# SSD decay matrices of a two-layer diffusion backbone: from rank-8 matmuls into PSUM to broadcast rows in SBUF

## The chip, the cores and the metric

The kernel runs on one core of a Trainium2 chip. The metric is the device time of one execution in microseconds; three runs of the kernel before gave a median of 1857.68 us (1857.05 to 1858.12). The profiled execution, from which all durations below come, took 1859.69 us, and its span from the first to the last instruction is 1858.0 us.

## The reference, cut to what matters

The model has two layers on 1024 latent and 256 context tokens of width 1024: layer 0 is windowed attention, layer 1 a bidirectional state-space mixer (SSD) with 8 groups of 4 heads of 64 and a state of 128. Only layer 1's scan is touched. For each direction, head and chunk of 128 tokens:

```python
a_cs = jnp.cumsum(da, axis=2)                        # running sum of dt * A inside a chunk
diff = a_cs[:, :, :, None] - a_cs[:, :, None, :]     # (query token q, source token s)
lmat = jnp.exp(jnp.where(lower, diff, -jnp.inf))     # decay from s to q, s <= q
cb = jnp.einsum('bcqgn,bcsgn->bcqsg', cm, bm)
y_diag = jnp.einsum('bcqsg,bcqsgr,bcsgrp->bcqgrp', cb, lmat, xdt)   # xdt = x * dt
y_off = jnp.einsum('bcqgn,bcgrpn,bcqgr->bcqgrp', cm, h_prev, jnp.exp(a_cs))
```

The backward direction does the same on the flipped sequence. The kernel puts both directions into one 128 x 128 matrix per head, with the source token on the partitions: where s is not after q the entry is exp(acs_f[q] + v_f[s]), elsewhere exp(acs_b[q] + v_b[s]), with v = ln(dt) - acs. Multiplied by cb this is M, and M times x gives y_diag of both directions.

## The kernel before, in words

Layer 0 fills about the first 755 us of the span, layer 1 the rest. Layer 1 starts with the constants (`ssd_consts`): dt for all 64 head-directions in two sets (768 and 512 tokens), the running sums `acs` by two scans on VectorE, `v`, and per chunk some small transposes by TensorE (lines 956, 959, 960) that ScalarE copies out (957, 961, 962). `rows()` splits `acs` and `v` each into a rounded high part (cast on ScalarE, 929) and the rest (subtraction on VectorE, 930), so that fp32r matmuls keep the precision, and SyncE stores both parts to DRAM (932).

Then comes the scan. 8 groups times 8 chunks are 64 slots, about 13.8 us each. A slot does the work of one chunk; between its steps `fill(0)` to `fill(4)` issue the projections of the next group (TensorE lines 1046, 1055, 1080, with weight loads on SyncE at 991, their split at 995 on ScalarE and 999 on VectorE), or in the last group the output projection. Beside that runs the chain of states of the next group (`states`: POOL xw 1130, TensorE 1153, POOL decay 1135, VectorE add 1165). The program is written in this order, but the order on each engine is set before the run by a list scheduler that models durations; on the chip each engine then takes its instructions strictly in that order, and a DMA is issued by SyncE in the place where the schedule has it.

The decays of a slot are made one slot ahead. `load_rows` reads 8 rows of acs and 16 of v (three small DMAs, 1176 and 1178) into `rraw`, of which there is one; `round_rows` casts it to fp32r on ScalarE (1181) and then loads the next. `decays` runs for two heads at a time: two matmuls (1189) with constant selecting rows give acs[q] + v[s] of both directions in one PSUM tile (`psX`, three buffers), VectorE copies the backward half over the forward half where `before` says so (1190), ScalarE takes the exponential (1191) into M. In the slot itself VectorE multiplies M by pcb (1205) and four matmuls use it (1230). Of the rest of a slot, these matter: POOL's xs and y (1225 to 1227) and the power (1242), the tail's transposes (1258) and their store uN (1260).

Of the kernel before, what the change touches and what calls it, by code (L numbers as in the profile page):

```python
# [9 lines left out]
F32 = mybir.dt.float32  # L10
BF16 = mybir.dt.bfloat16
F32R = mybir.dt.float32r
AF = mybir.ActivationFunctionType
ALU = mybir.AluOpType
# [3 lines left out]
P = 128  # L18
D = 1024
KT = D // P  # L20
LAT = 1024
# [11 lines left out]
G = 8  # L33
R = 4
HP = 64
NST = 128
NCH = LAT // P
# [5 lines left out]
    pj=1, S=2, pt=2, pv=1,  # L43
    rope_b=2, qf=3, qh=3, ql=2, kHH=2, kLL=2, qs=2, sgt=2, sm=7, mx=2, nm=2, es=2, sums=2, ph=2, pl=2, co=1, ot=2,
    oraw=3, h1=2, h1k=8, wada=8, sqa=1,
    cacc=2, cctx=1, bT=2, cT=2, xn4=4, xn2=1, bn4=4, bn2=1, sz=2, xw=2, hf=2, hx=2, M=2, y2=1, xs=1, uT=2, pj2=2, psX=3, sk=2, dg=2,
)
VLAST = 0
G0 = 6
# [54 lines left out]
class Kernel:  # L104
# [13 lines left out]
    def t(self, pool, shape, dt, tag, bufs=None):  # L118
        self.n += 1
        kw = {"bufs": bufs or BUFS.get(tag, 1)}  # L120
        return pool.tile(shape, dt, tag=tag, name=f"{tag}_{self.n}", **kw)
# [727 lines left out]
    def ssd_consts(self, p):  # L849
        nc, t, a = self.nc, self.t, self.a  # L850
        ps = self.psA
        NT = NCH + NCC
        dr = self.dr
# [12 lines left out]
        self.eacs = t(p, [P, NCH, 64], F32, "eacs")  # L866
        self.dtdec = t(p, [P, NT, 64], F32, "dtdec")
        self.dtb = t(p, [P, NCH, 32], F32, "dtb")
        self.eal = t(p, [P, 64, NT], F32, "eal")

        self.acs_d = t(dr, [2, 64, LAT], F32, "acs")
        self.v_d = t(dr, [2, 64, LAT], F32, "vrow")
        self.before = t(p, [P, P], mybir.dt.int32, "before")
        nc.vector.memset(self.before, 1)
        nc.gpsimd.affine_select(out=self.before, in_=self.before, pattern=[[-1, P]], compare_op=ALU.is_gt, fill=0, base=0, channel_multiplier=1)
# [1 line left out]
        q = self.pdt  # L877
# [19 lines left out]
        for i in (2, 0, 1):  # L897
            n = TT[i][1]
            pj = self.proj(ps, (wh, wl), i, tag="psX", m=64)
            nc.scalar.activation(dts[:, where[i] : where[i] + n], pj[:64, :n], AF.Identity, bias=db)  # L900
        for lo, n, chunks in ((0, 768, (0, 1, 2, 3, 8, 9)), (768, 512, (4, 5, 6, 7))):
            nb = n // P
            dt = dts[:, lo : lo + n]
            if lo:
                q = self.pool("dtp2", ctx=self.cdt, side="right")
            w1, w2, w3 = [t(q, [64, n], F32, x) for x in ("w1", "w2", "w3")]

            nc.vector.scalar_tensor_tensor(w1, in0=dt, scalar=-1.0, in1=dt, op0=ALU.mult, op1=ALU.min)
            nc.scalar.activation(w1, w1, AF.Exp)
            nc.vector.tensor_scalar_add(w2, w1, 1.0)  # L910
            nc.vector.tensor_scalar_add(w3, w2, -1.0)
            nc.vector.tensor_sub(w1, w1, w3)
            nc.scalar.activation(w2, w2, AF.Ln)
            nc.scalar.activation(w3, w2, AF.Exp, scale=-1.0)
            nc.vector.tensor_mul(w1, w1, w3)
            nc.vector.tensor_add(w1, w1, w2)
            nc.vector.scalar_tensor_tensor(dt, in0=dt, scalar=0.0, in1=w1, op0=ALU.max, op1=ALU.add)
            ln = w2
            nc.vector.tensor_scalar_max(ln, dt, 1.0e-38)
            nc.scalar.activation(ln, ln, AF.Ln)  # L920
            da = w1
            nc.vector.tensor_scalar(out=da, in0=dt, scalar1=al, scalar2=None, op0=ALU.mult)
            acs = w3
            nc.vector.tensor_tensor_scan(out=acs[:32], data0=keep[:32, :n], data1=da[:32], initial=0.0, op0=ALU.mult, op1=ALU.add)
            nc.vector.tensor_tensor_scan(out=acs[32:, ::-1], data0=keep[32:, :n][:, ::-1], data1=da[32:, ::-1], initial=0.0, op0=ALU.mult, op1=ALU.add)
            def rows(dst, src):
                h = t(q, [64, 512], F32R, "rowh", 2)
                l = t(q, [64, 512], F32R, "rowl", 2)
                nc.scalar.copy(h, src[:, :512])
                nc.vector.tensor_sub(l, src[:, :512], h)  # L930
                for x, y in enumerate((h, l)):
                    nc.sync.dma_start(dst[x, :, chunks[0] * P : chunks[0] * P + 512], y.bitcast(F32))

            rows(self.acs_d, acs)
            av = acs.rearrange("p (c n) -> p c n", n=P)
            tot = t(q, [64, 6], F32, "tot")[:, :nb]
            nc.vector.tensor_copy(tot[:32], av[:32, :, P - 1])
            nc.vector.tensor_copy(tot[32:], av[32:, :, 0])
            et = t(q, [64, 6], F32, "et")[:, :nb]
            nc.scalar.activation(et, tot, AF.Exp)  # L940
            nc.sync.dma_start(eal_d[0][:, chunks[0] : chunks[0] + 4], et[:, :4])
            if nb > 4:
                nc.sync.dma_start(eal_d[0][:, 8:10], et[:, 4:])

            nc.vector.tensor_sub(ln, ln, acs)
            rows(self.v_d, ln)

            dd = w1
            nc.vector.tensor_sub(dd.rearrange("p (c n) -> p c n", n=P), tot.unsqueeze(2).broadcast_to([64, nb, P]), av)
            nc.scalar.activation(dd, dd, AF.Exp)  # L950
            nc.vector.tensor_mul(dd, dd, dt)
            nc.scalar.activation(acs, acs, AF.Exp)
            for b, c in enumerate(chunks):
                sl = slice(b * P, (b + 1) * P)
                pt = t(ps, [P, 256], F32, "psX")
                nc.tensor.transpose(pt[:, 0:64], dd[:, sl], self.ident[:64, :64])
                nc.scalar.copy(self.dtdec[:, c, :], pt[:, 0:64])
                if c < NCH:
                    nc.tensor.transpose(pt[:, 64:128], acs[:, sl], self.ident[:64, :64])
                    nc.tensor.transpose(pt[:, 128:192], dt[:, sl], self.ident[:64, :64])  # L960
                    nc.scalar.copy(self.eacs[:, c, :], pt[:, 64:128])
                    nc.scalar.copy(self.dtb[:, c, :], pt[:, 160:192])
        nc.sync.dma_start(self.eal, eal_d.broadcast_to([P, 64, NT]))

    def taps(self, x, raw, acc, lo, hi, n):
# [130 lines left out]
    def ssd(self, c0):  # L1096
        nc, t, a = self.nc, self.t, self.a
        ps = self.psA
# [6 lines left out]
        ps2 = self.pool("scan", ctx=c0)  # L1105


        rraw = t(ps2, [32, 6, P], F32, "rraw")
        rrow = t(ps2, [P, 6, P], F32R, "rrow")
        nc.sync.dma_start(rraw, a["rrow"].rearrange("p (r n) -> p r n", r=6))  # L1110
        nc.vector.memset(rrow.bitcast(F32), 0.0)
        ys = []
        for x in range(2):
            y = t(ps2, [P, 260], F32, f"y{x}")
# [4 lines left out]
        def hd(d, g):  # L1119
            return slice(32 * d + 4 * g, 32 * d + 4 * g + 4)  # L1120
# [48 lines left out]
                        st["hb"][o] = h = hn  # L1169
                yield  # L1170

        def load_rows(n):
            g, c = divmod(n, NCH)
            cs = slice(c * P, (c + 1) * P)
            ar = self.acs_d.rearrange("h (d k) n -> (h d) k n", d=2)[:, 4 * g : 4 * g + 4, cs]
            nc.sync.dma_start(rraw[0:4, :4], ar)
            for d in range(2):
                nc.sync.dma_start(rraw[4 + 8 * d : 12 + 8 * d, 4 + d], self.v_d[:, hd(d, g), cs])

        def round_rows(n):  # L1180
            nc.scalar.copy(rrow[:32], rraw)
            if n + 1 < G * NCH:
                load_rows(n + 1)

        def decays(n, M, half):

            o = t(ps, [P, 512], F32, "psX").rearrange("p (d r n) -> p d r n", d=2, r=2)
            for d in range(2):
                nc.tensor.matmul(o[:, d], rrow[:, 4 + d], rrow[:, 2 * half : 2 * half + 2], start=True, stop=True)
            nc.vector.copy_predicated(o[:, 0], self.before.unsqueeze(1).broadcast_to([P, 2, P]), o[:, 1])  # L1190
            nc.scalar.activation(M[:, 2 * half : 2 * half + 2], o[:, 0], AF.Exp)

        def slot(n, st, M, fill, tick, last):

            g, c = divmod(n, NCH)
            cs = slice(c * P, (c + 1) * P)
            xc = X(st, c).rearrange("p (r h) -> p r h", r=R)
            if n + 1 < G * NCH:
                round_rows(n + 1)
            pcb = t(ps, [P, 512], F32, "psX")[:, :P]  # L1200
            nc.tensor.matmul(pcb, st["bT"][:, cs], st["cT"][:, cs], start=True, stop=True)
            po = t(ps, [P, 512], F32, "psX")
# [28 lines left out]
            if self.tail is not None:  # L1231
                self.tail(t(ps, [P, 512], F32, "psX"))
            fill(1)
            nM = None
            if n + 1 < G * NCH:
                nM = t(ps2, [P, R, P], F32, "M")
                decays(n + 1, nM, 0)
            nc.vector.tensor_add(yv, yv, yd[:, :256].rearrange("p (r h) -> p r h", r=R))
            nc.vector.tensor_mul(yf, yf, st["sz"][c])
            ss = t(ps2, [P, 1], F32, "ss", 2)  # L1240
            nc.scalar.activation(y2.rearrange("p d r h -> p (d r h)")[:, :257], y[:, :257], AF.Square, scale=1.0 / 16.0, accum_out=ss)
            nc.gpsimd.tensor_tensor(ss, ss, self.half, op=ALU.pow)
            fill(2)
            if nM is not None:
                decays(n + 1, nM, 1)
            nc.scalar.activation(yf, yf, AF.Copy, scale=ss)
            if c < NCH - 2:
                st["xw"] = xweight(st, g, c + 1, 0)
# [15 lines left out]

        post = Queue()
        st = {}
        load_rows(0)
        done = 0.0
        chain = None
        for cost in self.front(0, st, post):  # L1270
# [8 lines left out]
        post.flush()  # L1279
        for _ in chain:  # L1280
            pass
        M = t(ps2, [P, R, P], F32, "M")
        round_rows(0)
        for half in range(2):
            decays(0, M, half)
        st["xw"] = xweight(st, 0, 0, 0)
        self.tail = None
        with ExitStack():
            for g in range(G):
# [25 lines left out]
                for c in range(NCH):  # L1315
                    def fill(x):
                        run(total * (c + sum(SEGS[: x + 1]) / sum(SEGS)) / NCH)
# [233 lines left out]
def layout(i):  # L1551
# [31 lines left out]
    rm = np.where(k > q, np.float32(NEG), np.float32(0))  # L1583
    z = np.zeros((P, P), np.float32)

    rr = np.zeros((32, 6, P), np.float32)
    for x in range(4):
        for r in range(R):
            rr[4 + 4 * x + r, r] = 1.0
        rr[x, 4 + x % 2] = 1.0  # L1590
    d["rrow"] = rr.reshape(32, -1)
    d["mask"] = np.concatenate([lm, z, rm, z, z, lm, z, z, z], 1).astype(np.float32)
    w = i["ssd_w_in"][0]
    d["w_z"] = np.ascontiguousarray(w[:, :SW].reshape(2, 4, P, G, 256).transpose(3, 0, 2, 1, 4)).reshape(G, 2, P, 1024)
# [27 lines left out]
```

## Time and profile before

| | before |
|---|---|
| median of 3 runs | 1857.68 us |
| profiled execution, its span | 1859.69 us, 1858.0 us |
| TensorE busy, share of the span | 1778.6 us, 96% |
| VectorE, ScalarE, GpSimd busy | 63%, 49%, 39% |
| mean granted TensorE clock | 0.988 |
| DMA traffic | 196.30 MB, 106 GB/s |

PE is TensorE's matmul, PEld its weight load, DVE VectorE, ACT ScalarE, POOL GpSimd, SP (or SPq) SyncE, which issues most DMAs. A row of a group reads: line, engine, operation, output<-input, shape, count | busy us, mean ns of one | idle us of the engine just before them, and what ended it. Matmuls are pipelined, so a matmul's duration is longer than the distance to the next one; what it costs TensorE is that distance, from the starts in the timeline.

### The profile page before, as it was taken

How to read it: one execution, taken by the hardware profiler on the slowest of the kernel's cores; microseconds unless marked ns; L12 is line 12 of the kernel's file. 1: busy time of each engine (PE TensorE's matmuls, PEld its weight loads, DVE VectorE, ACT ScalarE, POOL GpSimd, SP SyncE). 2: the span in 40 equal slices, each digit the busy share in tenths (PEclk: the TensorE clock that was granted, in tenths of full speed). 3: DMA queues.
4: the chain of work that ended last, by engine and by line, in shares of the span. 5: the costliest groups of instructions: out<-in, count | busy, mean ns of one | idle time of the engine just before them, and what ended most of it. 6: DMA issues, size and time to landing. Idle time of an engine off the chain costs nothing. (4 is left out here: it accounts for less than half of the span.)

```text
span 1858.0 us, 29740 instructions
## 1 busy us (share of the span) xinstructions
PE 1778.6 (96%) x10684; PEld 1537.0 (83%) x10684; DVE 1176.4 (63%) x2208; ACT 902.9 (49%) x1858; POOL 731.7 (39%) x1007
## 2 busy tenths in 40 slices
PE   6999999999999998979999999999999999999997
PEld 4797877788898786768898898989889898988886
DVE  3654438777778666773766657576665757754743
ACT  3522336677788664552444435344443534543532
POOL 2441137654466454103252443525344352542411
PEclk9999999999999999989999999999999999999998
DMA  7767866443355447021111111111111111433552
GB/s 294 278 170 251 272 167 151 106 116 97 90 136 121 127 129 229 17 65 35 30 40 52 33 47 33 48 33 39 53 34 47 34 47 34 155 109 98 176 161 72
DMA packets 145492, 196.30 MB, mean 106 GB/s; under 512 B 15393, under 2 KB 84897, under 8 KB 144321
## 3 DMA queue, kind: packets, MB, share of 16 engines
q1 hardware_dynamic: 111280, 175.76, 30.2%
q0 software_dynamic: 34064, 18.65, 5.5%
q8 instruction: 84, 1.38, 0.3%
q14 instruction: 64, 0.52, 0.1%
HBM read 158.73 MB, written 35.92 MB: 105 GB/s over the span
## 5 line engine op out<-in xcount | busy, mean ns | idle before, releaser
L226 PE MATMUL pj<-uH,wh 128*128 128x256 f32 (+1 forms) x664 | 236.9, 357 | 5.7 <-DVE xn L1510 1.9
L228 PE MATMUL pj<-uH,wl 128*128 128x256 f32 (+1 forms) x664 | 224.5, 338 | 2.0 <-POOL wl L214 2.0
L227 PE MATMUL pj<-uL,wh 128*128 128x256 f32 (+1 forms) x664 | 224.1, 337 | 0.4 <-POOL uL L720 0.4
L1130 POOL TENSOR_TENSOR xw<-xn,dtdec 128x256 f32<-128x256 f32 x144 | 105.9, 738 | 205.4 <-PE psD L1153 102.9
L214 POOL TENSOR_TENSOR wl<-wr,wh 128x512 fp32r<-128x512 f32 x100 | 132.1, 1324 | 109.7 <-ACT wh L212 103.6
L1055 PE MATMUL pj<-uH,wh 128*128 128x512 f32 x512 | 171.7, 405 | 1.3 <-ACT xn L1022 1.3
L1055 PE MATMUL pj<-uH,wl 128*128 128x512 f32 x512 | 171.5, 404 | 0.0
L1055 PE MATMUL pj<-uL,wh 128*128 128x512 f32 x512 | 168.6, 399 | 0.0
L1080 PE MATMUL pj<-wh,uH 128*128 128x256 f32 x512 | 154.7, 302 | 0.0
L702 DVE TENSOR_TENSOR pl<-pt,ph 128x512 fp32r<-128x512 f32 x168 | 114.3, 688 | 59.7 <-ACT ph L701 58.9
L1080 PE MATMUL pj<-wh,uL 128*128 128x256 f32 x512 | 151.2, 295 | 0.0
L1080 PE MATMUL pj<-wl,uH 128*128 128x256 f32 x512 | 150.9, 295 | 0.0
L226 PEld LDWEIGHTS pj<-uH,wh 128*128 128x128 f32 x664 | 126.3, 190 | 28.8 <-issue 7.8
L212 ACT CAST wh<-wr 128x512 fp32r<-128x512 f32 (+1 forms) x140 | 89.8, 643 | 106.2 <-PE pj L227 78.1
L228 PEld LDWEIGHTS pj<-uH,wl 128*128 128x128 f32 x664 | 125.9, 190 | 17.7 <-POOL wl L214 3.2
L676 DVE CUSTOM_DVE_ANT_0 sm<-S,mask,nsink 128x640 f32<-128x640 f32 (+2 forms) x160 | 119.0, 772 | 33.7 <-PE S L673 19.7
L1259 ACT ACTIVATE uT<-psX,nw 128x128 f32<-128x128 f32 x128 | 47.0, 367 | 189.7 <-PE psX L1258 188.6
L227 PEld LDWEIGHTS pj<-uL,wh 128*128 128x128 f32 x664 | 126.6, 191 | 11.3 <-issue 1.1
L701 ACT CAST ph<-pt 128x512 fp32r<-128x512 f32 x168 | 97.6, 586 | 60.9 <-PE pt L697 54.9
L678 ACT ACTIVATE sm<-sm,nm 128x640 f32<-128x640 f32 (+2 forms) x160 | 118.5, 742 | 17.4 <-DVE nm L676 14.6
L1225 POOL TENSOR_TENSOR xs<-xn,sk 128x256 f32<-128x256 f32 x64 | 42.1, 657 | 185.1 <-DVE sk L1221 183.8
L1055 PEld LDWEIGHTS pj<-uL,wh 128*128 128x128 f32 x512 | 95.6, 188 | 19.9
(332 smaller groups left out, 5022.6 us busy)
## 6 DMA issues: line engine op xcount, KB each, us to landing
wr<-w_x SPq DMA_DIRECT2D x32, 512.0 KB
wr<-wo SPq DMA_DIRECT2D x48, 256.0 KB
wr<-w_sk SPq DMA_DIRECT2D x24, 512.0 KB
wr<-wg SPq DMA_DIRECT2D x44, 256.0 KB
qs<-q POOLq DMA_DIRECT2D x40, 256.0 KB, 3.9
wada<-w_ad SPq DMA_DIRECT2D x8, 1024.0 KB
wr<-wq SPq DMA_DIRECT2D x32, 256.0 KB
wl<-w_ada SPq DMA_DIRECT2D x32, 256.0 KB
```

The source lines that it names most:

```text
L212: nc.scalar.copy(h, raw)
L214: (eng or nc.vector).tensor_tensor(l, raw, h, op=ALU.subtract)
L226: self.nc.tensor.matmul(ps, lh, rh, start=first and i == 0, stop=False)
L227: self.nc.tensor.matmul(ps, lh, rl, start=False, stop=False)
L228: self.nc.tensor.matmul(ps, ll, rh, start=False, stop=last and i == n - 1)
L676: nc.vector.tensor_tensor_reduce(out=sm[:, :W], in0=Sv, in1=self.mask[:, m0 : m0 + W], scale=-SCALE, scalar=self.nsink[:, 4 * j + r : 4 * ...
L678: nc.scalar.activation(sm[:, :W], sm[:, :W], AF.Exp, bias=nm[:, r : r + 1], scale=-1.0, accum_out=sums[:, r : r + 1])
L701: nc.scalar.copy(ph, ptf)
L702: nc.vector.tensor_sub(pl, ptf, ph)
L1055: nc.tensor.matmul(raw[:, 512 * i : 512 * i + 512], l[:, k, :], r[i][:, k, :], start=k + y == 0, stop=k == KT - 1 and y == 2)
L1080: nc.tensor.matmul(pj[:, c], l, r[:, k, :], start=c % 2 + q + k + y == 0, stop=c % 2 == 1 and q == 1 and k == 3 and y == 2)
L1130: nc.gpsimd.tensor_tensor(xw, X(st, c).rearrange("p (r h) -> p r h", r=R), self.dtdec[:, c, hd(d, g)].unsqueeze(2).broadcast_to([P, R, HP] ...
```

## The change

The running sums are stored to DRAM unsplit, v is not stored, and `rows()` is gone with its casts, subtractions and its second and third stores per set. The constants get one more transpose per latent chunk (8 in all, line 955 in the new file), of v: the forward part is copied to `vf` by ScalarE (956), and `vo` = v_b - v_f is formed by VectorE (957).

For each slot two DMAs of 256 KB now bring four rows of acs (512 B each), repeated on all 128 partitions: `fd` forward (two buffers, issued two slots ahead, in the program right after `fill(1)`) and `bd` backward (one buffer, issued one slot ahead, right after the exponentials of the slot before). GpSimd adds vo to bd in place (`offset`, 1173); one copy_predicated of 128 x 512 in SBUF puts bd over fd (1178); four exponentials of 128 x 128, one per head, with vf as the bias of each partition, finish M in place in fd (1180). The matmuls of 1189, the selecting rows, the casts of 1181 and the two PSUM tiles a slot are gone.

```diff
-    cacc=2, cctx=1, bT=2, cT=2, xn4=4, xn2=1, bn4=4, bn2=1, sz=2, xw=2, hf=2, hx=2, M=2, y2=1, xs=1, uT=2, pj2=2, psX=3, sk=2, dg=2,
+    cacc=2, cctx=1, bT=2, cT=2, xn4=4, xn2=1, bn4=4, bn2=1, sz=2, xw=2, hf=2, hx=2, fd=2, bd=1, y2=1, xs=1, uT=2, pj2=2, psX=3, sk=2, dg=2,
...
-            def rows(dst, src):
-                h = t(q, [64, 512], F32R, "rowh", 2)
-                l = t(q, [64, 512], F32R, "rowl", 2)
-                nc.scalar.copy(h, src[:, :512])
-                nc.vector.tensor_sub(l, src[:, :512], h)
-                for x, y in enumerate((h, l)):
-                    nc.sync.dma_start(dst[x, :, chunks[0] * P : chunks[0] * P + 512], y.bitcast(F32))
-
-            rows(self.acs_d, acs)
+            nc.sync.dma_start(self.acs_d[0][:, chunks[0] * P : chunks[0] * P + 512], acs[:, :512])
...
             nc.vector.tensor_sub(ln, ln, acs)
-            rows(self.v_d, ln)
...
                     nc.scalar.copy(self.dtb[:, c, :], pt[:, 160:192])
+                    nc.tensor.transpose(pt[:, 192:256], ln[:, sl], self.ident[:64, :64])
+                    nc.scalar.copy(self.vf[:, c, :], pt[:, 192:224])
+                    nc.vector.tensor_sub(self.vo[:, c, :], pt[:, 224:256], self.vf[:, c, :])
...
-        def load_rows(n):
+        fwd, bwd = {}, {}
+
+        def load_rows(n, d):
+            if n < G * NCH:
+                g, c = divmod(n, NCH)
+                x = (fwd, bwd)[d][n] = t(ps2, [P, R, P], F32, ("fd", "bd")[d])
+                nc.sync.dma_start(x, self.acs_d[:, hd(d, g), c * P : (c + 1) * P].broadcast_to([P, R, P]))
+
+        def offset(n):
             g, c = divmod(n, NCH)
-            cs = slice(c * P, (c + 1) * P)
-            ar = self.acs_d.rearrange("h (d k) n -> (h d) k n", d=2)[:, 4 * g : 4 * g + 4, cs]
-            nc.sync.dma_start(rraw[0:4, :4], ar)
-            for d in range(2):
-                nc.sync.dma_start(rraw[4 + 8 * d : 12 + 8 * d, 4 + d], self.v_d[:, hd(d, g), cs])
-
-        def round_rows(n):
-            nc.scalar.copy(rrow[:32], rraw)
-            if n + 1 < G * NCH:
-                load_rows(n + 1)
-
-        def decays(n, M, half):
-
-            o = t(ps, [P, 512], F32, "psX").rearrange("p (d r n) -> p d r n", d=2, r=2)
-            for d in range(2):
-                nc.tensor.matmul(o[:, d], rrow[:, 4 + d], rrow[:, 2 * half : 2 * half + 2], start=True, stop=True)
-            nc.vector.copy_predicated(o[:, 0], self.before.unsqueeze(1).broadcast_to([P, 2, P]), o[:, 1])
-            nc.scalar.activation(M[:, 2 * half : 2 * half + 2], o[:, 0], AF.Exp)
+            nc.gpsimd.tensor_tensor(bwd[n], bwd[n], self.vo[:, c, 4 * g : 4 * g + 4].unsqueeze(2).broadcast_to([P, R, P]), op=ALU.add)
+
+        def decays(n):
+            g, c = divmod(n, NCH)
+            x = fwd.pop(n)
+            nc.vector.copy_predicated(x, self.before.unsqueeze(1).broadcast_to([P, R, P]), bwd.pop(n))
+            for r in range(R):
+                nc.scalar.activation(x[:, r], x[:, r], AF.Exp, bias=self.vf[:, c, 4 * g + r : 4 * g + r + 1])
+            load_rows(n + 1, 1)
+            return x
...
             fill(1)
+            load_rows(n + 2, 0)
             nM = None
             if n + 1 < G * NCH:
-                nM = t(ps2, [P, R, P], F32, "M")
-                decays(n + 1, nM, 0)
+                offset(n + 1)
...
             fill(2)
-            if nM is not None:
-                decays(n + 1, nM, 1)
+            if n + 1 < G * NCH:
+                nM = decays(n + 1)
```

The scheduler orders all engines anew, so instructions move. In the constants, TensorE before has its 26 small transposes (each printed as a matmul with `ident`) as one block behind the stream of projections; a part of it:

```order
L1055 MATMUL pj_2228_9147<-uH_2144_8675,wl_9087 128x512
L956 MATMUL psX_8882<-ident_63,w_2177_8840 128x64
L956 MATMUL psX_8889<-ident_63,w_2177_8840 128x64
L956 MATMUL psX_8896<-ident_63,w_2177_8840 128x64
L959 MATMUL psX_8882<-ident_63,w_2179_8842 128x64
L960 MATMUL psX_8882<-ident_63,dt_8761 128x64
L959 MATMUL psX_8889<-ident_63,w_2179_8842 128x64
```

The same place in the changed program, again TensorE (lines 948, 951 and 952 are the old 956, 959 and 960; 1050 is the old 1055):

```order
L948 MATMUL psX_8872<-ident_63,w_2178_8841 128x64
L948 MATMUL psX_8882<-ident_63,w_2178_8841 128x64
L948 MATMUL psX_8892<-ident_63,w_2178_8841 128x64
L1050 MATMUL pj_2222_9149<-uL_2145_8676,wh_9087 128x512
L1050 MATMUL pj_2222_9149<-uH_2057_8255,wl_9089 128x512
L1050 MATMUL pj_2222_9149<-uH_2144_8675,wl_9089 128x512
L1050 MATMUL pj_2222_9149<-uH_2057_8255,wh_9087 128x512
L1050 MATMUL pj_2222_9149<-uH_2144_8675,wh_9087 128x512
L1050 MATMUL pj_2222_9149<-uL_2058_8256,wh_9087 128x512
L1050 MATMUL pj_2222_9149<-uL_2145_8676,wh_9087 128x512
```

Two more projections follow there before the first 951; the later transposes stand in eight more pieces between projections and conversions.

SyncE in the second group of slots, before (wr is a weight load, uN a store of a slot's output):

```order
L991 DMA wr_10852<-w_x 128x1024
L1260 DMA uN_2146_8709<-uT_10268 128x2x128
L1176 DMA rraw_8997<-acs_8739 4x4x128
L1178 DMA rraw_8997<-vrow_8740 8x1x128 x2
L1260 DMA uN_2146_8709<-uT_10398 128x2x128
```

And in the changed program:

```order
L1249 DMA uN_2146_8709<-uT_10239 128x2x128
L1169 DMA fd_10379<-acs_8741 128x4x128
L1169 DMA bd_10564<-acs_8741 128x4x128
L986 DMA wr_10803<-w_x 128x1024
L1249 DMA uN_2146_8709<-uT_10364 128x2x128
L1169 DMA fd_10535<-acs_8741 128x4x128
L1169 DMA bd_10717<-acs_8741 128x4x128
```

The two broadcasts take the place of the three small loads, between the same weight loads and stores, in one queue.

GpSimd in the changed program, about the same time (1214 to 1216 are the old 1225 to 1227, 1121 the old 1130, 1126 the old 1135; before, the row of 1173 has no counterpart):

```order
L1121 TENSOR_TENSOR xw_10310<-xn_2290_9724,dtdec_8736 128x256
L1121 TENSOR_TENSOR xw_10325<-xn_2290_9724,dtdec_8736 128x256
L1173 TENSOR_TENSOR bd_10564<-bd_10564,vo_8739 128x512
L1215 TENSOR_TENSOR y_2198_9000<-y_2424_10485 128x256
L1214 TENSOR_TENSOR xs_10499<-xn_2204_9011,sk_10502 128x256
L1121 TENSOR_TENSOR xw_10403<-xn_2204_9011,dtdec_8736 128x256
L1216 TENSOR_TENSOR y_2198_9000<-y_2198_9000,xs_10499 128x256
L1126 TENSOR_TENSOR hf_2409_10409<-hx_10329,eal_8740 128x256
```

The offset now stands in the same queue as the slot's y and the chain of states, ahead of them where the schedule had it ready first.

More of the change, by code (lines that the diff above doesn't have):

```diff
@@ L868, in ssd_consts @@
         self.dtb = t(p, [P, NCH, 32], F32, "dtb")
+        self.vf = t(p, [P, NCH, 32], F32, "vf")
+        self.vo = t(p, [P, NCH, 32], F32, "vo")
         self.eal = t(p, [P, 64, NT], F32, "eal")
-        self.acs_d = t(dr, [2, 64, LAT], F32, "acs")
-        self.v_d = t(dr, [2, 64, LAT], F32, "vrow")
+        self.acs_d = t(dr, [1, 64, LAT], F32, "acs")
         self.before = t(p, [P, P], mybir.dt.int32, "before")
@@ L1105, in ssd @@
         ps2 = self.pool("scan", ctx=c0)
[L1108 to L1111, printed above, removed]
         ys = []
@@ L1197, in slot @@
             xc = X(st, c).rearrange("p (r h) -> p r h", r=R)
-            if n + 1 < G * NCH:
-                round_rows(n + 1)
             pcb = t(ps, [P, 512], F32, "psX")[:, :P]
@@ L1266, in ssd @@
         st = {}
-        load_rows(0)
+        load_rows(0, 0)
+        load_rows(0, 1)
+        load_rows(1, 0)
         done = 0.0
@@ L1281, in ssd @@
             pass
[L1282 to L1285, printed above, removed]
+        offset(0)
+        M = decays(0)
         st["xw"] = xweight(st, 0, 0, 0)
@@ L1584, in layout @@
     z = np.zeros((P, P), np.float32)
[L1586 to L1591, printed above, removed]
     d["mask"] = np.concatenate([lm, z, rm, z, z, lm, z, z, z], 1).astype(np.float32)
```

## The prediction

> **What bounds the kernel now.** I read the windows first, since the page's shares mix two layers. Columns are length, then busy time (and instructions) of PE, PEld, DVE, ACT and POOL, the granted clock, DMA share and GB/s. The scan lies between 870 and 1755 us.
>
> ```profile
> 760.00:870.00 110.00, 97.62 (x556) 84.05 (x555) 74.84 (x102) 55.84 (x97) 11.72 (x18) 0.92 0.14 38
> 1000.00:1130.00 130.00, 129.51 (x806) 116.35 (x805) 88.94 (x164) 59.84 (x122) 48.20 (x73) 1.00 0.16 45
> 1130.00:1260.00 130.00, 129.51 (x807) 116.40 (x806) 87.11 (x160) 56.76 (x116) 52.20 (x78) 1.00 0.14 39
> 1520.00:1650.00 130.00, 127.92 (x785) 114.30 (x785) 89.69 (x161) 61.86 (x123) 53.34 (x77) 1.00 0.31 96
> 1650.00:1755.00 105.00, 103.86 (x506) 86.51 (x505) 61.20 (x105) 47.74 (x92) 36.55 (x43) 1.00 0.42 130
> ```
>
> In the scan TensorE is busy 129.5 of 130 us at full clock; no other engine is above 90 of 130. The waits of the same stretch, by engine, say the same from the other side: nearly everything waits for TensorE, and the only TensorE waits of note are those for xw (the chain of states) of 3.4 and 4.8 us in 885.
>
> ```profile
> DVE psX L1190 <- PE psX L1189: 69.1, 47, 4.2
> DVE M L1205 <- PE psX L1201: 36.4, 22, 2.6
> PEld psD L1153 <- POOL xw L1130: 4.8, 7, 0.7
> DVE M L1205 <- ACT M L1191: 4.0, 7, 1.3
> PE psD L1153 <- POOL xw L1130: 3.4, 7, 0.5
> ```
>
> So in the scan TensorE's issue time is the time. The constants stage ahead of it is the exception (760 to 870: 97.6 of 110 us, clock 0.92), and there the change also works.
>
> **What the change removes from TensorE.** The groups, with columns of busy us, mean ns | idle before:
>
> ```profile
> L1189 PE MATMUL psX<-rrow 128*128 128x256 f32 x256 | 53.5, 290 | 0.0
> L1230 PE MATMUL psX<-xn,M 128*128 128x64 f32 x512 | 64.9, 267 | 0.8 <-DVE dg L1219 0.8
> ```
>
> The 290 ns are latency, not cost: the matmuls overlap. The timeline gives the cost as the distance between starts.
>
> ```profile
> 1194.13 0.40 PE L1189 MATMUL psX<-rrow 128*128 128x256 f32 x2
> 1194.36 0.28 PE L1080 MATMUL pj<-wl,uH 128*128 128x256 f32 x1
> ...
> 1196.49 0.40 PE L1189 MATMUL psX<-rrow 128*128 128x256 f32 x2
> 1196.72 0.40 PE L1055 MATMUL pj<-uH,wh 128*128 128x512 f32 x1
> ```
>
> A pair takes 0.23 us, the same pace as the stream around it (0.12 us each). 256 / 2 x 0.23 = 29.4 us; the first four fall into the constants stage, among other gaps, so I count 252 / 2 x 0.23 = **29.0 us off**. This is not hidden by anything: TensorE's queue goes straight on with projections. Reading the 53.5 us of busy time as the gain would be the upper error.
>
> **The constants.** Eight transposes of 64 columns come in. Their nearest row is the one at 0.11 us distance and half clock below: 8 x 0.11 = 0.9, at full clock half of it; I take **+0.5**. More is in the order. Before, TensorE stands still between the first three transposes and the next, then works at half clock (timeline, then windows):
>
> ```profile
> 793.37 0.39 PE L956 MATMUL psX<-ident,w 64*128 64x64 f32 x3 [0.84 <-DVE w L951]
> 800.66 0.36 PE L959 MATMUL psX<-ident,w 64*128 64x64 f32 x1 [6.90 <-ACT dtdec L957]
> 800.82 0.31 PE L960 MATMUL psX<-ident,dt 64*128 64x64 f32 x1
> 800.93 0.31 PE L959 MATMUL psX<-ident,w 64*128 64x64 f32 x1
> ```
>
> ```profile
> 793.00:801.00 8.00, 0.73 (x6) 0.60 (x7) 6.60 (x11) 5.61 (x11) 0.00 (x0) 0.65 0.42 127
> 801.00:809.00 8.00, 7.63 (x41) 6.75 (x40) 7.82 (x10) 6.48 (x27) 0.00 (x0) 0.50 0.28 71
> ```
>
> Lost: 0.84 + 6.90 us of idling, and up to half of the next 8.00 us at clock 0.50, 4.0, together at most 11.7 us. After, nine projections of 512 columns stand between the same instructions, and two casts and two subtractions per set are gone from the chain that ScalarE and VectorE work off. Against that, the exponential that overwrites acs in place must now wait until the unsplit store has read it, and this store sits behind a weight load on SyncE; eight new copies of vf and subtractions of vo stand in the same chain. Nothing recovered (0) and everything (-11.7) are the ends; since both effects are of the size of the stall, I take **-5**. [...]
>
> **What the other engines pay, and whether TensorE sees it.** Per slot:
>
> ```profile
> L1181 ACT CAST rrow<-rraw 32x768 fp32r<-32x768 f32 x64 | 52.8, 825 | 16.7 <-PE psX L1189 13.2 <-ACT M L1191 2.8 <-DMA rraw<-vrow 0.5
> L1190 DVE COPY_PREDICATED psX<-before,psX 128x256 f32<-128x256 int32 x128 | 54.1, 424 | 69.6 <-PE psX L1189 69.1
> L1191 ACT ACTIVATE M<-psX 128x256 f32<-128x256 f32 x128 | 47.1, 369 | 13.6 <-DVE psX L1190 13.4
> L1259 ACT ACTIVATE uT<-psX,nw 128x128 f32<-128x128 f32 x128 | 47.0, 367 | 189.7 <-PE psX L1258 188.6
> L1205 DVE TENSOR_TENSOR M<-M,psX 128x512 f32<-128x512 f32 x64 | 43.8, 684 | 41.1 <-PE psX L1201 36.4 <-ACT M L1191 4.0 <-PE pj L1470 0.7
> L214 POOL TENSOR_TENSOR wl<-wr,wh 128x512 fp32r<-128x512 f32 x100 | 132.1, 1324 | 109.7 <-ACT wh L212 103.6 <-PE pj L228 2.6 <-ACT es L682 2.3
> L1130 POOL TENSOR_TENSOR xw<-xn,dtdec 128x256 f32<-128x256 f32 x144 | 105.9, 738 | 205.4 <-PE psD L1153 102.9 <-ACT xn L1022 89.8 <-PE psX L1210 12.7
> ```
>
> ScalarE: 0.825 + 2 x 0.369 = 1.56 us go, four exponentials of 128 columns come; the nearest shape is uT's at 0.367, so 1.47. About nothing. VectorE: 2 x 0.424 = 0.85 go, one copy of 512 columns comes, nearest L1205's 0.684. GpSimd: one add of 128 x 512, 1.32 by the row of wl: 64 x 1.32 = 85 us more. In the windows it is busy 52 of 130 us and a slot is 885 / 64 = 13.8 us (64 is the count of L1205), so it rises from 5.5 to 6.8 us a slot. None of the three becomes the bound.
>
> What can reach TensorE is lateness. M now comes from one copy and four exponentials in a row (0.7 + 1.5 = 2.2 us) where the last half took 0.42 + 0.37 = 0.8, so M is 1.4 us later. Cover: the product with pcb waited for M 4.0 us in all but for TensorE's pcb 36.4, and the matmuls that use M (L1230) waited 0.8 us in the whole run. In the slot of the timeline above M was done 7.6 us ahead:
>
> ```profile
> 1200.27 0.68 DVE L1205 TENSOR_TENSOR M<-M,psX 128x512 f32<-128x512 f32 x1
> ...
> 1208.56 0.67 PE L1230 MATMUL psX<-xn,M 128*128 128x64 f32 x5
> ```
>
> If that cover were 1.4 us short in a tenth of the slots it would cost 6 x 1.4 = 9 us; I count this with the next term.
>
> The transfers: two of 256 KB a slot. 512 KB in 13.8 us is 38 GB/s, on top of 39 to 45 at a share of 0.14 to 0.16, and of 130 at 0.42 in the last group; engines are not the limit, latency is. The nearest row with the same shape (256 KB in runs of 512 B) lands 3.9 us after issue:
>
> ```profile
> qs<-q POOLq DMA_DIRECT2D x40, 256.0 KB, 3.9
> 1201.12 0.41 SPq L991 DMA_DIRECT2D wr<-w_x  x1
> SPq L991 <- DVE wl L999: 130.6, 20, 16.8
> SPq L1260 <- ACT uT L1259: 250.4, 45, 8.5
> SPq L1176 <- ACT M L1191: 60.9, 32, 17.7
> ```
>
> fd has two slots, 27 us. bd has one buffer, so a loop: copy_predicated 0.7, issue 0.4, landing 3.9, offset 1.3, together 6.3 of 13.8 us; 7.5 us are left. It stands in SyncE's queue behind weight loads and stores that wait themselves: 20 times for VectorE's wl, 6.5 us on average and 16.8 at most. The small loads of before stood in the same queue with one buffer too, and L1189 waited 0.0 us. That bounds the new wait from below at 0. From above: the 130.6 us of waits for wl, if all of it were passed on. A third path is GpSimd's own queue: the offset waits for bd and VectorE, and xw for the states is behind it. It takes 1.32 us in front of an xw in each slot; TensorE waits for xw only 14 times today, 8.2 us with the weight loads, so there is little stacked up but also no large reserve shown. Half a slot's offset in one slot of ten is 64 x 0.1 x 0.66 = 4 us. For all new waits together I take **+3**, ends 0 and about 30.
>
> GpSimd is also slowed by VectorE:
>
> ```profile
> 1144.61 1.61 POOL L1130 TENSOR_TENSOR xw<-xn,dtdec 128x256 f32<-128x256 f32 x1
> ...
> 1144.53 1.22 DVE L999 TENSOR_TENSOR wl<-wr,wh 128x1024 fp32r<-128x1024 f32 x1
> 1147.68 0.62 POOL L1135 TENSOR_TENSOR hf<-hf,eal 128x256 f32<-128x256 f32 x1
> ```
>
> 1.61 us instead of about 0.6 beside a subtraction of two SBUF inputs: an offset may take 2.3 us, and the new copy_predicated, now all in SBUF, may hold GpSimd for 0.7 us a slot. [...]
>
> **Sum.** 1858.0 - 29.0 + 0.5 - 5 + 3 = 1827.5 us of span. The profiled execution is 1.7 us longer than its span and 2.0 us longer than the median, so the median to expect is 1827.5 + 1.7 - 2.0 = **1827 us**. Its own range: with the stall regained whole and no wait 1858.0 - 29.0 + 0.5 - 11.7 = 1818; with nothing regained and waits of 8 us 1837.
>
> **Rivals.**
>
> *The offsets hold up the states.* If a third of the 64 offsets delay TensorE by 1.0 us (the contention) or so, 21 us come back and with nothing regained in the constants: 1858 - 28.5 + 21 = about 1850; half of it, 1840. For it: the row of 1.61 us, and the in-order queue. Against: xw runs a state ahead (two buffers), and GpSimd idles 60% of the scan.
>
> *The backward loads pace the slots: slower.* Place: SyncE's queue, a bd behind a weight load that waits for VectorE. Each us over the 7.5 of reserve stalls the copy, M and the matmuls of 1230, and all behind them on TensorE. If half of the 130.6 us arrives: 1858 - 34 + 65 = 1889. It decides from 34 us, a mean of 0.5 us a slot. For it: 16.8 us at most is beyond the reserve. Against: the mean of 6.5 is inside, and the loads of before had the same place.
>
> *No change.* The removed matmuls leave holes that the same TensorE queue cannot fill, since what follows waits for ScalarE or VectorE: 1858 give or take 3.7. Against it stand the waits view, where VectorE and ScalarE wait for TensorE, and 88 of 130 us of VectorE.
>
> *More than the forecast,* the whole stall and some of the other idle time between 760 and 870 us: 1812 to 1818.
>
> **How the numbers follow.** Forecast 1818 to 1837: 0.58. More: 0.06. Offsets hold up part: 0.19, 1837 to 1853. No change: 0.05. Slower: 0.12. Within 0.2%, 3.7 us, of the old time is what a measurement of this kernel hardly tells from none. Faster 0.58 + 0.06 + 0.19 = 0.83, same 0.05, slower 0.12. The range of 8 in 10 goes from 1814 to 1852; beyond it lie the slower and unchanged cases and a few hundredths.
>
> **What would show it.** In the changed profile: about 129.5 of 130 us of TensorE busy in the scan's windows, and no TensorE row waiting for M, bd or xw by more than a few us; slots of 13.8 - 0.45 = about 13.4 us; the gap before the second kind of transpose below 7 us. Wrong would be: waits of TensorE for xw (1144) or of copy_predicated for bd of tens of us, or a granted clock below 1.00 inside the scan.

## The result and the profile after

The change makes the kernel slower: 1980.83 us median (1978.99 to 1981.6, 4 runs) against 1857.9 us (1857.05 to 1861.69, 4 runs), a ratio of 1.0652 with a 95% interval of 1.0636 to 1.0667. Forecast was 1827 us. The profiled span is 1978.5 us, 120.5 more than before.

The windows of the changed kernel (same columns as before; the scan now lies between 870 and 1880 us):

```profile
1000.00:1130.00 130.00, 116.37 (x694) 101.39 (x692) 72.90 (x126) 48.35 (x112) 51.96 (x75) 0.97 0.29 72
1130.00:1260.00 130.00, 114.21 (x667) 99.49 (x668) 74.10 (x131) 44.94 (x105) 56.31 (x80) 0.96 0.23 66
...
870.00:1880.00 1010.00, 911.06 (x5217) 789.65 (x5217) 578.59 (x999) 377.20 (x860) 419.99 (x582) 0.96 0.31 85
```

TensorE, busy 129.5 of 130 us before, is now busy 114 of 130 and at clock 0.96. Over the scan it idles 1010 - 911 = 99 us, where it idled 885 - 879 = 6. No other engine has become full: VectorE and ScalarE are less busy than before, so this is waiting, not work. The waits of the same stretch:

```profile
POOL bd L1173 <- DMA bd<-acs: 273.5, 53, 10.2
ACT fd L1180 <- DVE fd L1178: 247.3, 44, 16.0
DVE y L1227 <- POOL y L1216: 127.4, 31, 6.9
...
DVE fd L1178 <- DMA fd<-acs: 86.7, 38, 5.8
...
PE psX L1199 <- POOL xw L1121: 34.1, 5, 7.5
...
PE psX L1192 <- DVE y L1227: 19.1, 20, 2.2
```

Read from below, there are two chains with one root. TensorE waits for VectorE's y (1227), that waits for GpSimd's y (1216), and TensorE waits for GpSimd's xw (1121), its longest wait; GpSimd's own large wait is the offset (1173) for the load of bd, 5.2 us each. The timeline shows the first chain (POOL, DVE, PE and SP rows of the changed kernel, put together in order of time):

```profile
1143.56 0.74 DVE L1178 COPY_PREDICATED fd<-before,bd 128x512 f32<-128x512 int32 x1 [5.27 <-DMA fd<-acs]
...
1144.37 0.36 SPq L1169 DMA_DIRECT2D bd<-acs  x1
...
1149.46 1.04 POOL L1173 TENSOR_TENSOR bd<-bd,vo 128x512 f32<-128x512 f32 x1 [3.76 <-DMA bd<-acs]
...
1150.45 0.72 POOL L1216 TENSOR_TENSOR y<-y,xs 128x256 f32<-128x256 f32 x1
...
1151.21 0.42 DVE L1227 TENSOR_TENSOR y<-y,psX 128x256 f32<-128x256 f32 x1 [6.34 <-POOL y L1216]
...
1151.69 0.70 PE L1192 MATMUL psX<-hf,cT 128*128 128x256 f32 x2 [1.14 <-DVE y L1227]
...
1153.79 1.00 PE L1219 MATMUL psX<-xn,fd 128*128 128x64 f32 x8
...
1159.55 0.73 POOL L1216 TENSOR_TENSOR y<-y,xs 128x256 f32<-128x256 f32 x1
...
1161.54 0.74 DVE L1178 COPY_PREDICATED fd<-before,bd 128x512 f32<-128x512 int32 x1
...
1162.35 0.36 SPq L1169 DMA_DIRECT2D bd<-acs  x1
...
1166.93 1.04 POOL L1173 TENSOR_TENSOR bd<-bd,vo 128x512 f32<-128x512 f32 x1 [6.65 <-DMA bd<-acs]
...
1170.30 1.72 POOL L1216 TENSOR_TENSOR y<-y,xs 128x256 f32<-128x256 f32 x1
```

The copy releases bd, SyncE issues the next load at once, it takes 5 us, for 3.8 of which GpSimd stands still, then comes the add to y that the slot's end is waiting for, then TensorE gets its PSUM tile back, and only after the y of the next slot (1159.55) comes the next copy. From one offset to the next are 17.5 us here. Slots differ; over the group of eight from the y at 1150.45 to the one at 1275.13 a slot takes 15.6 us on average, against 13.6 in the kernel before (108.5 us for eight).

The second chain is shorter. GpSimd and TensorE at another place:

```profile
1216.61 1.04 POOL L1173 TENSOR_TENSOR bd<-bd,vo 128x512 f32<-128x512 f32 x1 [4.64 <-DMA bd<-acs]
1217.60 0.61 POOL L1121 TENSOR_TENSOR xw<-xn,dtdec 128x256 f32<-128x256 f32 x1
...
1218.27 1.22 PE L1199 MATMUL psX<-xw,bn 128*128 128x256 f32 x2 [6.03 <-POOL xw L1121]
```

All five waits of this kind (34.1 us) are alike: the xw stands directly behind an offset before which GpSimd had stood still for 4.6 to 6.5 us.

The timeline does not name the slot that an instruction belongs to; the order does. Here is GpSimd in the changed program, the row numbers in front, xs_10225 being the xs of one slot n. bd_10286 is made for slot n + 2; bd_10176, for slot n + 1, stands further up:

```
499 L1173 TENSOR_TENSOR bd_10286<-bd_10286,vo_8739 128x512
500 L1231 TENSOR_TENSOR ss_10159<-ss_10159,half_8733 128x1
501 L1214 TENSOR_TENSOR xs_10225<-xn_2204_9011,sk_10228 128x256
502 L1215 TENSOR_TENSOR y_2198_9000<-y_2372_10217 128x256
503 L1216 TENSOR_TENSOR y_2198_9000<-y_2198_9000,xs_10225 128x256
```

In the code the offset of slot n + 1 follows slot n's y. In the order the offset of n + 2 comes before it. I call the number of y that an offset runs past its lead: 0 is the code's order; the changed kernel has a lead of 2 for 53 of 64 offsets and 3 for 8, among them the one at 1149.46 us above.

### The profile page after: what moved, and what is told of

It reads as the page before. It is cut to its first block, busy times and chain, and to the rows that moved or that the text cites. A ratio compares the mean times of both kernels' runs of the same rounds, so it can differ in the third digit from the quotient of the medians.

```text
span 1978.5 us, 29286 instructions
## 1 busy us (share of the span) xinstructions
PE 1802.8 (91%) x10436; PEld 1530.8 (77%) x10436; DVE 1169.2 (59%) x2147; ACT 880.5 (45%) x1926; POOL 796.9 (40%) x1071
## 5 line engine op out<-in xcount | busy, mean ns | idle before, releaser
L1173 POOL TENSOR_TENSOR bd<-bd,vo 128x512 f32<-128x512 f32 x64 | 67.4, 1053 | 329.7 <-DMA bd<-acs 283.4
L1180 ACT ACTIVATE fd<-fd,vf 128x128 f32<-128x128 f32 x256 | 83.0, 391 | 255.5 <-DVE fd L1178 255.3
L1050 PE MATMUL pj<-uH,wl 128*128 128x512 f32 x512 | 167.4, 402 | 0.0
L1121 POOL TENSOR_TENSOR xw<-xn,dtdec 128x256 f32<-128x256 f32 x144 | 91.1, 637 | 151.7 <-PE psX L952 86.1
L226 PEld LDWEIGHTS pj<-uH,wh 128*128 128x128 f32 x664 | 127.6, 192 | 29.9 <-issue 8.1
L227 PEld LDWEIGHTS pj<-uL,wh 128*128 128x128 f32 x664 | 127.7, 192 | 11.3 <-issue 1.1
L1050 PEld LDWEIGHTS pj<-uH,wh 128*128 128x128 f32 x512 | 95.4, 191 | 24.0 <-ACT bn L1017 5.9
```

Source lines behind the costliest of these rows:

```text
L226: self.nc.tensor.matmul(ps, lh, rh, start=first and i == 0, stop=False)
L227: self.nc.tensor.matmul(ps, lh, rl, start=False, stop=False)
L1050: nc.tensor.matmul(raw[:, 512 * i : 512 * i + 512], l[:, k, :], r[i][:, k, :], start=k + y == 0, stop=k == KT - 1 and y == 2)
L1121: nc.gpsimd.tensor_tensor(xw, X(st, c).rearrange("p (r h) -> p r h", r=R), self.dtdec[:, c, hd(d, g)].unsqueeze(2).broadcast_to([P, R, HP] ...
```

## The experiments

Five theories were tried: A, the loop of the single bd buffer; B, fd arriving late on VectorE; C, GpSimd's added work and its contention with VectorE; D, the load on the DMA engines; E, the place in the queues, a waiting instruction put ahead of work that was ready.

**More buffers.**

```diff
-fd=2, bd=1,
+fd=2, bd=2,
-            load_rows(n + 1, 1)
+            load_rows(n + 2, 1)
+        load_rows(1, 1)            # before the scan
```

> bd has two buffers and is loaded two slots ahead; all else as in the changed kernel (1981 us). Theory A, the backward load's loop (one buffer, 4.9 us to land, GpSimd's offset waiting for it with the slot's y behind): the 273 us of waits of the offset for bd go, and most of the 122 us loss with them, 1840 to 1880 us. Theory B, fd too late on VectorE (86.7 us of waits): little, above 1940. Theory C, GpSimd's extra 1.05 us a slot and its contention with VectorE: little, above 1950. Theory D, the transfers' load on the DMA engines: none, about 1980.

1949.92 us, ratio 1.0483 (1.0462 to 1.0504).

> fd has three buffers and is loaded three slots ahead; bd stays as it is. A: VectorE's waits for fd go, the offset still waits, above 1930 us. B: 1850 to 1890. C and D: about 1980.

The edit is the same for fd (three buffers, `load_rows(n + 3, 0)`): 1978.99 us, ratio 1.0639 (1.0621 to 1.0656).

> Both of the above; to make room uT and hx have one buffer instead of two. A: as with bd alone or somewhat less, 1830 to 1870 us. A and B together: about 1830, near the forecast. C or D: above 1940.

1953.29 us, ratio 1.0500 (1.0472 to 1.0529). A and B both fall in the form in which they were stated. The waits of the kernel with two bd buffers say why:

```profile
POOL bd L1173 <- DMA bd<-acs: 243.6, 54, 9.3
...
DVE y L1227 <- POOL y L1216: 104.6, 32, 6.3
```

The offset waits as before although its load has a buffer more. In the order of these kernels the lead has grown with the buffers: 3 for 51 offsets with two bd buffers, 4 for 50 with both. The scheduler has pulled the offset one slot further ahead, and it still waits 4.5 us each time with two bd buffers, against 5.2.

**The load on the DMA engines.** Two broadcast loads a slot were added to the kernel before (the diff leaves out their calls, and that uT and hx have one buffer):

```diff
+            nc.sync.dma_start(t(ps2, [P, R, P], F32, 'tr'), self.acs_d[0:1][:, hd(d, g), c * P : (c + 1) * P].broadcast_to([P, R, P]))
```

> The kernel before, with two broadcast loads of 256 KB a slot into a scratch tile that nothing reads, issued by SyncE where the changed kernel issues its loads (uT and hx with one buffer, for room). D: the kernel before becomes slower by tens of us, 1900 or more. A, B and C: within 10 us of the kernel before, since nothing waits for the data.

2176.73 us, ratio 1.1705 (1.1688 to 1.1722), but this says nothing about D: with nothing to wait for, the schedule issued the loads ahead of need, the last at 1413.9 us, and SyncE itself waited for the one scratch buffer. Its waits between 870 and 1880 us:

```profile
SPq L1182 <- DMA tr<-acs: 462.1, 112, 5.8
```

and two windows of the same kernel, during the loads and after them:

```profile
1130.00:1260.00 130.00, 66.97 (x360) 58.82 (x359) 38.16 (x71) 23.63 (x48) 20.75 (x33) 0.76 0.28 71
...
1700.00:1900.00 200.00, 199.51 (x1258) 180.32 (x1257) 130.29 (x243) 85.29 (x172) 80.30 (x122) 1.00 0.16 47
```

What it shows is what a blocked SyncE queue does: 67 of 130 us of TensorE and clock 0.76 while it lasts, and the old pace once it is over. The second attempt copies from DRAM to DRAM into four places in turn and ties each pair behind the slot's store.

```diff
+                with self.tc.issue_after(store.ins):
+                    nc.sync.dma_start(x, self.acs_d[0:1][:, hd(d, g), c * P : (c + 1) * P].broadcast_to([P, R, P]))
```

> The kernel before, with two broadcast copies of 256 KB a slot from acs in DRAM to DRAM in runs of 512 B, issued by SyncE right behind the slot's store, into four places in turn, so that SyncE seldom waits for them. D: 1900 us or more. A, C and E: within 15 us of the kernel before.

1874.12 us, ratio 1.0082 (1.0059 to 1.0106). That is 14.6 us (11 to 20 by the interval), and nearly all of it after 1650 us: TensorE keeps 259.0 of 260 us from 870 to 1130, as before, and 114.7 of 120 from 1650 to 1770, where before it kept 103.9 of 105 from 1650 to 1755. D explains about an eighth of the loss, as far as a copy to DRAM stands for a load to SBUF. The kernels with ties below speak more plainly, since they make the same loads as the changed kernel.

**The place in the queues.** `issue_after` ties an instruction behind another in its own engine's queue, without a wait.

```diff
-            nc.gpsimd.tensor_tensor(yv, yv, xs, op=ALU.add)
+            yadd = nc.gpsimd.tensor_tensor(yv, yv, xs, op=ALU.add)
...
-                offset(n + 1)
+                with self.tc.issue_after(yadd.ins):
+                    offset(n + 1)
```

> Only the place of the offset in GpSimd's queue changes: it is tied behind the slot's last add to y (1216), one bd buffer as in the changed kernel. Theory E, the schedule places an instruction where its model has the load landed, the load lands later, and what stands behind waits: the offset no longer holds y, the waits of VectorE's y for GpSimd (127 us) go, 1880 to 1930 us, the rest stays with the copies on VectorE that wait for loads. Theory C, GpSimd's added work and contention: above 1960. Theory D, load on the DMA engines: above 1960.

1841.18 us, ratio 0.9900 (0.9872 to 0.9927): 140 us less than the changed kernel by one tie, with the same buffers, loads and arithmetic. The scheduler orders the rest anew around the tie, so other instructions moved too. The lead is 0 for all 64. More came back than I expected: VectorE's waits of the copy for fd (86.7 us) went as well.

```diff
-            nc.vector.tensor_mul(yf, yf, st["sz"][c])
+            ymul = nc.vector.tensor_mul(yf, yf, st["sz"][c])
...
-                nM = decays(n + 1)
+                with self.tc.issue_after(ymul.ins):
+                    nM = decays(n + 1)
```

> As the run before, and the copy on VectorE is tied behind the slot's product with sz, so that neither queue waits for a load ahead of the slot's own y. E: 1830 to 1870 us if one bd buffer leaves the load enough time. A, the single buffer: still above 1920. C and D: above 1950.

With both ties 1831.7 us, ratio 0.9848 (0.9826 to 0.9870). This is below both kernels, 1.5% less than the kernel before. Its windows, the second over the whole scan:

```profile
1130.00:1260.00 130.00, 129.29 (x789) 115.01 (x788) 89.87 (x155) 56.28 (x132) 65.52 (x91) 1.00 0.29 81
...
870.00:1740.00 870.00, 864.08 (x5183) 765.24 (x5182) 594.89 (x998) 382.65 (x864) 433.72 (x580) 1.00 0.36 100
```

The offset's group (busy us, mean ns | idle before), and the load in the table of DMA issues (count, size, us to landing):

```profile
L1173 POOL TENSOR_TENSOR bd<-bd,vo 128x512 f32<-128x512 f32 x64 | 66.8, 1044 | 4.0 <-DMA bd<-acs 3.8
```

```profile
bd<-acs SPq DMA_DIRECT2D x64, 256.0 KB, 5.4
```

The load takes 5.4 us to land here, longer than in the changed kernel (4.9), and the offset waits 3.8 us in the whole run instead of 283. TensorE idles 6 us in the scan, as before the change. The timeline of this kernel, SyncE and GpSimd:

```profile
1149.21 0.36 SPq L1169 DMA_DIRECT2D bd<-acs  x1
...
1153.64 0.74 POOL L1216 TENSOR_TENSOR y<-y,xs 128x256 f32<-128x256 f32 x1
...
1154.96 1.04 POOL L1173 TENSOR_TENSOR bd<-bd,vo 128x512 f32<-128x512 f32 x1 [0.58 <-DMA bd<-acs]
```

> As the run before with two bd buffers, loaded two slots ahead. E alone: like the run before, 1825 to 1865 us. A and E together, the buffer matters once the order is right: at least 20 us below the run before. C and D: above 1950.

1835.7 us, ratio 0.9869 (0.9851 to 0.9887): a second buffer gains nothing once the order is right, so one buffer was enough.

**Which tie matters, and which engine.** The copy alone tied, and, in another kernel, nothing tied but the offset on VectorE (`nc.vector.tensor_tensor` for `nc.gpsimd.tensor_tensor`):

> The changed kernel with only the copy on VectorE tied behind the slot's product with sz; the offset stays where the schedule put it, ahead of the slot's last add. E: GpSimd's wait for bd is the one that costs, so little is gained, 1930 to 1975 us, and the slot's y still waits for GpSimd. If instead the copy's own waits for loads (86.7 us) were the cost: below 1880.

1871.11 us, ratio 1.0062 (1.0047 to 1.0077). I had expected little gain, and 110 us came back. The order explains it: tying the copy also delays the load that it releases, and so the offset; its lead is now 1 for 63 of 64. The offset still waits, but only the next slot's y is behind it. The waits of this kernel's scan:

```profile
POOL bd L1173 <- DMA bd<-acs: 224.7, 55, 6.6
...
PE psD L1144 <- POOL xw L1121: 8.9, 6, 1.7
...
PE psX L1199 <- POOL xw L1121: 7.8, 2, 6.2
```

So the sum of the offset's waits (224.7 here, 273.5 in the changed kernel) is not the loss: TensorE idles 2.7 of the 130 us from 1130 to 1260 here, against 15.8 in the changed kernel. That what counts is whether the wait lies in the loop of a slot is argued from the order; no run shows it apart.

> The changed kernel with the offset on VectorE, nothing tied. C, GpSimd's work and contention: below 1880 us. E: the instruction that waits for bd now stands in VectorE's queue and holds what is behind it there: above 1930.

1960.61 us, ratio 1.0543 (1.0527 to 1.0559). VectorE now stands still for bd (172.6 us in 60 waits), with the same lead of 2 for 54 offsets, counted against VectorE's own y (1227). C falls: taking the work off GpSimd helps by 20 us of 123, and with the ties GpSimd does all of it in a kernel that is faster than before.

| kernel | most offsets' lead | median us |
|---|---|---|
| changed | 2 | 1980.83 |
| two bd buffers | 3 | 1949.92 |
| three fd buffers | 3 | 1978.99 |
| both | 4 | 1953.29 |
| offset on VectorE | 2 | 1960.61 |
| copy tied | 1 | 1871.11 |
| offset tied | 0 | 1841.18 |
| both tied | 0 | 1831.7 |
| both tied, two bd buffers | 0 | 1835.7 |
| both tied, and one in the constants (below) | 0 | 1861.3 |

From a lead of 2 on the time is 1950 to 1981 us and more lead changes little; with 1 it is just above that of before, and with 0 below it, except in the last kernel, where another tie was added. Why two bd buffers still gain 31 us was not followed up.

The copy on VectorE has a lead as well, counted against VectorE's y (1227): 1 for 55 of 64 in the changed kernel, 2 for 54 with three fd buffers, 0 for all wherever the copy is tied, and 0 for 41 and 1 for 23 with the offset alone tied. In these runs the two leads fall together. They show that the order of the offset and the copy costs the time, and do not divide the loss between the two.

**The constants.**

```diff
+            behind = ExitStack()
+            if lo:
+                behind.enter_context(self.tc.issue_after(copied.ins))
             et = t(q, [64, 6], F32, "et")[:, :nb]
...
+            behind.close()
...
-                    nc.scalar.copy(self.vf[:, c, :], pt[:, 192:224])
+                    copied = nc.scalar.copy(self.vf[:, c, :], pt[:, 192:224])
```

> Both ties as before (1832 us), and in the constants ScalarE's work on the second set of tokens, from the exponential of the totals on, is tied behind the first set's copies out of PSUM. The 9 to 10 us of TensorE's gaps between the small transposes (2.0, 5.4 and 2.9) shrink if ScalarE's order is their cause: 1822 to 1829 us. If the chain on VectorE is: 1832 or more.

1861.3 us, ratio 1.0014 (1.0002 to 1.0026). The gap behind ScalarE shrank from 5.38 to 1.45 us, and another before the next transposes, behind VectorE's bT, grew from 2.88 to 6.95: the stall has moved behind VectorE's chain there. The 30 us by which this kernel is slower than with the two ties alone lie elsewhere: the schedule behind the tie differs, and in the scan TensorE is busy 121.2 of 130 us between 1520 and 1650. Which row does that was not followed up, so this run does not decide what the constants could gain.

## Why the prediction was wrong, point by point

**What TensorE saves** was about right, as far as the kernel with both ties shows it: its span is 1832.5 us, 25.5 less than before, where 28.5 were forecast for the matmuls less the eight transposes. In the changed kernel itself nothing of it can be seen.

**New waits, +3 us with ends 0 and about 30,** is the term that failed. In its place stand 120.5 + 28.5 = 149 us: 93 us more of idle TensorE in the scan (99 against 6), and by estimate 45 us by which the same matmuls keep TensorE busy longer: 174.6 ns each (911.06 / 5217) against 166.1 before without those of 1189, at a clock of 0.96 against 1.00. The rest, about 11 us, is not accounted for. Two steps led there. The loop of bd was counted from copy to copy, 6.3 of 13.8 us, with 7.5 us of reserve. The length was about right, 0.74 + 0.36 + 4.9 + 1.04 = 7.0. But it was taken as closed in itself: I did not ask which slot's work stands behind the offset in GpSimd's queue. With a lead of 2 or 3 the y of an earlier slot lies in the same loop. In the stretch above, the offset (1.0 us), the way from the y behind it to the next copy (11.1) and the way from that copy to the next offset (5.4) follow one another, and these are the 17.5 us. The forward load, which I had given 27 us and no term, is part of the delay too: the copy waited 5.27 us for it there, and 86.7 us in the scan. The order that would have told this was at hand; I read in it that the offset stands ahead of y, and not that it belongs to the slot after next. And the lower bound, that the old loads with one buffer cost L1189 nothing, was no bound: there the waiting instruction was a cast in ScalarE's queue, and what stood behind it, I had not looked at either.

**The rival of the backward loads** had the right sign, and a chance of 0.12, but the wrong place: SyncE issued bd 0.07 us after the copy ended (1144.30 to 1144.37), not behind weight loads. The rival of the offsets, with 0.19, had the right place, GpSimd's queue, and a right victim, xw: it costs TensorE 34.1 of its 99 idle us, and y 19.1 directly. Its cause and price were wrong: not 1.0 us of contention, but the offset's wait for its load, 5.2 us each time, and five waits of TensorE of 6.8 us. Of the signs that were to show the forecast wrong, the waits for xw (at 1199 and not at 1144) and the clock below 1.00 came; the copy waited for bd only 5.7 us, because GpSimd's offset stood in front of it and took that wait. In the case for little stacked up, the 14 waits and 8.2 us for xw are most likely seven waits counted twice, as seen by the weight load and by the matmul.

**The constants, -5,** were 0. Before, TensorE's gaps there were 0.84, 6.90, 1.05 and 1.30 us; after, the stall went to another transpose, as TensorE's timeline of the changed kernel shows:

```profile
802.71 0.27 PE L951 MATMUL psX<-ident,w 64*128 64x64 f32 x1 [2.01 <-ACT dtdec L949]
...
808.66 0.74 PE L955 MATMUL psX<-ident,w 64*128 64x64 f32 x3 [5.38 <-ACT dtb L954]
...
812.28 1.11 PE L1014 MATMUL pj<-ident,bT 128*128 128x128 f32 x4 [2.88 <-DVE bT L975]
```

10.3 us against 10.1, and the clock from 760 to 870 us is 0.92 as before. Projections put between the transposes moved the place of the stall and did not make it shorter.

**The prices of the instructions** were near: the offset 1.05 us (1.32 taken), the copy 0.76 (0.68), an exponential 0.39 (0.37), a load 4.9 us to land (3.9). None of these errors matters beside the order.

**Contention** between GpSimd and VectorE did not show as a loss: xw took 637 ns on average, and 651 with both ties, against 738 before. Single instructions do stretch (1.60 us for a decay at 1143.18 us in the kernel with both ties, beside VectorE's subtraction wl<-wr,wh from 1142.64 to 1144.31, against 0.62 for the decay at 1157.49), but that kernel is the fastest.

**The clock** I had as a bound on long stalls in the constants only. In the scan, five waits of TensorE for xw take 34.1 us, 6.8 each, and the clock is 0.96. Behind the wait of 6.03 us shown above the windows of the changed kernel read:

```profile
1218.00:1222.00 4.00, 3.73 (x15) 3.55 (x16) 2.43 (x3) 0.00 (x0) 3.35 (x6) 0.50 0.11 32
1222.00:1230.00 8.00, 8.00 (x55) 7.78 (x54) 4.66 (x7) 3.19 (x9) 1.70 (x2) 0.82 0.23 56
1230.00:1236.00 6.00, 6.00 (x51) 5.90 (x51) 0.43 (x2) 0.91 (x4) 3.39 (x6) 1.00 0.06 16
```

The clock is 0.50 in the 4 us behind this gap, 0.82 in the next 8 and 1.00 after them. The gaps and the lower clock both go away with the ties: with both, no wait in TensorE's list for the scan is longer than 0.6 us, and the clock is 1.00.

## What to carry to other kernels

Where a scheduler fixes the order of each engine, a load in front of an instruction is not only a latency to hide (4.9 us in the changed kernel) but a place in a queue (one tie on the offset was worth 140 us): ask which unit of work each waiting instruction belongs to, and which earlier unit's work it stands ahead of. Count that lead from the order before pricing anything. If it is not zero, tie the instruction to its place; here more buffers let the order run further ahead and gave back at most 31 of 123 us.

## What was not expected of the hardware

A broadcast load of 256 KB in rows of 512 B took 4.8 to 4.9 us from issue to landing in the changed kernel and 5.1 to 5.4 with both ties, where the slots are shorter, against 3.9 for a load of the same size from GpSimd's queue before. And two copies of this size a slot, from DRAM to DRAM, that nobody waits for cost the kernel before 14.6 us, nearly all after 1650 us, in the last group and the tail. What in that stretch makes them cost time was not followed up.
